# New landing and issue times in the list scheduler of a hybrid SSD / RG-LRU / retention / RWKV-7 block (one Trainium2 core)

## The chip, the cores and the metric

The kernel runs on one core of a Trainium2 chip. The metric is the device time of one execution in microseconds, the median of several runs. The engines are named as in the profile: PE is TensorE (PEld its weight loads), DVE is VectorE, ACT is ScalarE, POOL is GpSimd, SP is SyncE, whose queue (SPq) issues almost all transfers.

## The reference, cut to what matters

One layer over 512 tokens of width 1024, in float32. A combined input projection feeds four token mixers and their gates; the mixer outputs are projected, gated, summed and projected again; a convolutional FFN follows.

```python
def hybrid_mixer(h, w_in, ssm_p, lru_p, ret_p, rwkv_p, w_branch, w_out, cos, sin):
    proj = h @ w_in
    (m_z, m_xbc, m_dt, l_gate, l_x, r_q, r_k, r_v, r_g, rw, gate_logits) = jnp.split(proj, ...)
    y_ssd = mamba2_branch(m_z, m_xbc, m_dt, *ssm_p)
    y_lru = rglru_branch(l_gate, l_x, *lru_p)
    y_ret = retention_branch(r_q, r_k, r_v, r_g, *ret_p, cos, sin)
    y_rwkv = rwkv7_branch(rw, *rwkv_p)
    ys = jnp.stack([y_ssd, y_lru, y_ret, y_rwkv], axis=2)
    branch = jnp.einsum('bsmw,mwd->bsmd', ys, w_branch)
    merged = jnp.sum(jax.nn.sigmoid(gate_logits) * branch, axis=2)
    return merged @ w_out

x = x + hybrid_mixer(rms_norm(x, norm_mix), ...)
x = x + (silu(gt) * val) @ w_down          # val, gt: causal conv of rms_norm(x) @ w_up
return rms_norm(x, norm_final)
```

The RWKV-7 recurrence (a state of 64 x 64 per head, 16 heads) is the sequential part.

## The kernel before, in words

**The products.** Every large product is done in three fp32r matmuls (high x high, high x low, low x high). A weight block of 128 x 1024 floats is loaded by SP (`raw`, L469, three buffers), split on ACT into `whi` (L463) and on DVE into `wlo` (L464), and multiplied by `mm3` (L482, L483, L484) or its counterparts in `proj_tokens` (L603 to L605) and `tail_product` (L1317 to L1319) into an `acc` bank of PSUM, of which there are three. These products are called the large products below.

**The RWKV part.** It goes over eight pairs of heads, j = 0 to 7. `rwkv_a1(j)` makes the projections and decays (L654 to L706). `rwkv_a2(j)` makes 64-token blocks: on DVE and POOL the operands `g` and `bk` (L717 on POOL, L718 to L721 on DVE), on PE their products (L735), on ACT and DVE the masked copies (`ab` L737, `g` L738, `gb` L739), then transposes of `bk` and `v` on PE (L459 `ra<-ident,bk` and `ra<-ident,pv`). A triangular solve follows: `ab` goes through DRAM (`nd` L780, `nt` L783), DVE does 31 steps of two instructions (L789, L791), and the result goes through DRAM again: four writes `xd` (L797), four writes `xtd` (L798), two reads `xr` (L803), four reads `tt` (L806). `rwkv_b(j)` uses it: small matmuls L817 from `xr` and `ab`, a copy on ACT (L821), small matmuls L827 from `tt` and `xr`, a copy on ACT (L830), and then a chain over eight chunks, PE L840, DVE L842, PE L844, ACT L845 and DVE L846, PE L848, DVE L851, and L840 of the next chunk.

**What fills.** Beside the RWKV part stand, in this order of the program, the other mixers (`lru_tiles`, `ret_pair`, `mamba_group`, at last `mamba_finish`), and when they are done and their pool `fl` is closed, `branch` for three of the mixers: it reads the mixer outputs back (`yr`, L1240), splits them (`yh`, `yl`) and does the gate and branch products. The mixer outputs are written to DRAM by `spill` (L609, `y`). After the RWKV part come the last branch, the output product, the FFN and the last norm.

**What sets the order.** The program only lists instructions. At the end of the build `_order` (L406) makes the order of every engine: `_graph` collects dependences, tiles and pools, `_run` (L238) is a list scheduler that plays the program with a duration for each instruction (`_cost`, L115) and takes on each engine the ready instruction of the highest priority; on PE a small matmul that is ready goes before a large product. `_latest` turns the resulting times into new priorities, this is done `_RUNS` = 8 times, and the order with the smallest end is fixed on all engines. The scheduler's times are nowhere in the program; only the order is. For a transfer `_run` has two numbers: how long the issue occupies SP (450 ns before) and when the data has landed (an issue of 450 ns, the bytes at 330 per ns on one shared wire, then 1,500 ns, or 2,500 ns for reads of five kinds of scratch: `xd`, `xtd`, `y`, `ym`, `acd`). For POOL it stretches a two-input DVE instruction that runs beside a POOL one.

Of the kernel before, what the change touches and what calls it, by code (L numbers as in the profile page):

```python
# [66 lines left out]
_RUNS = 8  # L67
_HOP = 60.0
_SWITCH = 500.0
_BACK = 17.0  # L70


def _base(name):
    return name.rsplit("_", 1)[0]
# [163 lines left out]
def _run(g, prio, margin):  # L238


    import heapq
    import types
    E = mybir.EngineType
    ins, N, real = g.ins, g.N, g.real
    left = [len(p) for p in g.preds]
    est, start, done, dur_of = [0.0] * N, [0.0] * N, [0.0] * N, [0.0] * N
    engines = [E.PE, E.DVE, E.Activation, E.Pool, E.SP]
    free = {e: 0.0 for e in engines}
    pend, ready, order = {e: [] for e in engines}, {e: [] for e in engines}, {e: [] for e in engines}
    held, table, wire, was, run = [], "", 0.0, False, 1  # L250
    weights, shorts = [], []
    queue = {t: list(q) for t, q in g.queue.items()}
    room = {t: [(0.0, "")] * b for t, b in g.bufs.items()}
    n_users = {t: len(u) for t, u in g.users.items()}
    pool_left, pool_end = {}, {}
    for t, u in g.users.items():
        pool_left[g.pool_of[t]] = pool_left.get(g.pool_of[t], 0) + len(u)
    behind = {}

    def offer(k):  # L260

        for n in g.news[k]:
            if queue[g.tag_of[n]][0] != n or not room[g.tag_of[n]]:
                return False
            if any(pool_left.get(q, 0) for q in g.gates.get(g.pool_of[n], ())):
                return False
        for n in g.news[k]:
            queue[g.tag_of[n]].pop(0)
            at, old = heapq.heappop(room[g.tag_of[n]])
            est[k] = max(est[k], at)  # L270
            if old:
                behind.setdefault(k, []).append(old)
            for q in g.gates.get(g.pool_of[n], ()):
                est[k] = max(est[k], pool_end.get(q, 0.0))
        heapq.heappush(pend[g.eng[k]], (est[k], k))
        return True

    def try_held():
        again = True
        while again:  # L280
            again = False
            for k in list(held):
                if offer(k):
                    held.remove(k)
                    again = True

    for k in real:
        if not left[k]:
            if g.news[k]:
                held.append(k)  # L290
            else:
                offer(k)
    try_held()
    seq = []
    while len(seq) < len(real):
        best = None
        for e in engines:
            if ready[e] or (e == E.PE and (weights or shorts)):
                t = free[e]
            elif pend[e]:  # L300
                t = max(free[e], pend[e][0][0])
            else:
                continue
            if best is None or t < best[0]:
                best = (t, e)
        t, e = best
        while pend[e] and pend[e][0][0] <= t:
            k = heapq.heappop(pend[e])[1]
            heapq.heappush(ready[e], (-1.0 if g.lead.get(k, k) != k else prio[k], k))
        if e == E.PE:  # L310
            while ready[e]:
                k = heapq.heappop(ready[e])[1]
                heapq.heappush(weights if g.acc[k] else shorts, (-1.0 if g.lead.get(k, k) != k else prio[k], k))
            early = []
            while shorts and shorts[0][0] >= 0 and est[shorts[0][1]] + (300.0 if g.small[shorts[0][1]] else margin) > t:
                early.append(heapq.heappop(shorts))
            if weights and not shorts:
                k = heapq.heappop(weights)[1]
            else:
                if not shorts:  # L320
                    shorts, early = early, []
                    heapq.heapify(shorts)
                k = heapq.heappop(shorts)[1]
            for x in early:
                heapq.heappush(shorts, x)
        else:
            k = heapq.heappop(ready[e])[1]
        i = ins[k]
        dur, tail = g.cost[k]
        if e == E.Activation and type(i).__name__ == "InstActivation":  # L330
            sets = _TABLES.get(str(i.func).split(".")[-1])
            if sets and table not in sets:
                table = sets[0]
                dur += 1283.0
        if e == E.PE:
            if g.small[k] != was:
                was = g.small[k]
                dur += _SWITCH
            if not run and g.acc[k]:
                dur += _BACK  # L340
            run = run + 1 if g.acc[k] else 0
        if e == E.DVE and free[E.Pool] > t and len(i.ins) > 1 and not g.tiles_of[k][-1].startswith(("ra", "rb", "acc")):
            dur *= 1.0 + 0.7 * min(1.0, (free[E.Pool] - t) / dur)
        order[e].append(k)
        seq.append(k)
        start[k], dur_of[k] = t, dur
        free[e] = t + dur
        done[k] = t + dur + tail
        if type(i).__name__ == "InstDMACopy":
            free[e] = t + (450.0 if e == E.SP else 100.0)  # L350
            dur_of[k] = free[e] - t
            wire = max(wire, t + 450.0) + 4.0 * i.outs[0].bass_ap.size() / 330.0
            done[k] = wire + (2500.0 if i.outs[0].bass_ap.tensor.space != bass.MemoryType.DRAM and
                              _base(i.ins[0].bass_ap.tensor.name) in ("xd", "xtd", "y", "ym", "acd") else 1500.0)
        opened = bool(g.news[k])
        for s in g.succ[k]:
            left[s] -= 1
            est[s] = max(est[s], t if k in g.after[s] else t + dur if g.eng[s] == e and e != E.SP else done[k])
            if not left[s]:
                if g.news[s]:  # L360
                    held.append(s)
                    opened = True
                else:
                    offer(s)
        for m in g.tiles_of[k]:
            n_users[m] -= 1
            p = g.pool_of[m]
            pool_left[p] -= 1
            pool_end[p] = max(pool_end.get(p, 0.0), done[k])
            if not n_users[m]:  # L370
                heapq.heappush(room[g.tag_of[m]], (max(done[x] for x in g.users[m]), m))
                opened = True
        if opened:
            try_held()
    return types.SimpleNamespace(order=order, start=start, done=done, dur=dur_of, seq=seq, behind=behind, end=max(done))
# [30 lines left out]
def _order(tc, nc):  # L406

    PE = mybir.EngineType.PE  # L410
    g = _graph(nc)
    first = [float(k + g.N * g.acc[k]) for k in range(g.N)]
    prio, best = first, None
    for n in range(_RUNS):
        r = _run(g, prio, _MARGIN)
        if best is None or r.end < best.end:
            best = r
        late = _latest(g, r, [PE])
        prio = [first[k] if g.eng[k] == PE else late[k] for k in range(g.N)]
    behind = mybir.DependencyInfo(mybir.DependencyClass.NoSync, mybir.DependencyReason.DATA)  # L420
    for seq in best.order.values():
        for a, b in zip(seq, seq[1:]):
            tc.add_manual_dep(g.ins[b], g.ins[a].name, behind, reason="order of issue")
# [1121 lines left out]
```

## Time and profile before

| | |
|---|---|
| runs | 1572.96, 1568.45, 1569.73 us (median 1569.73) |
| profiled execution | 1573.08 us, its span 1571.3 us |
| PE busy | 1532.9 us, 98% |
| DVE / ACT / POOL busy | 1086.4 us, 69% / 734.9 us, 47% / 62.9 us, 4% |
| DMA | 169.46 MB, mean 108 GB/s |
| mean granted PE clock | 0.990 |

The profile is of one execution. Busy PE time counts every moment in which a matmul is under way; matmuls are pipelined, so two that follow each other overlap in the records, and a stretch in which they follow each other slowly is still busy. The distance between starts tells the pace. "DMA a<-b" in a wait means that the transfer's semaphore came last.

### The profile page before, as it was taken

The page shows a single profiled execution, that of the slowest core. Times are in us where ns is not written, and L with a number is a line of the kernel's source. Part 1 is how long each engine was busy: PE and PEld are TensorE (multiplying, and loading weights), DVE is VectorE, ACT ScalarE, POOL GpSimd, SP SyncE. Part 2 cuts the span into 40 slices and gives each one's busy share as a digit, 9 for nine tenths or more (in the row PEclk, how much of TensorE's full clock was granted, in tenths as well). Part 3 has the DMA queues.
Part 4 walks back from the last instruction along what each step waited for, and adds up shares of the span by engine and source line. Part 5 has one row for each costly group of instructions (what it writes and reads, how often), then busy time and mean ns, then how long its engine had stood idle before and what let it go on. Part 6 is the DMA issues. An engine that isn't in the chain of part 4 may idle for free.

```text
span 1571.3 us, 22179 instructions
## 1 busy us (share of the span) xinstructions
PE 1532.9 (98%) x8324; PEld 1286.6 (82%) x8324; DVE 1086.4 (69%) x2334; ACT 734.9 (47%) x1198; POOL 62.9 (4%) x78
## 2 busy tenths in 40 slices
PE   7999999999999999998999999999999999999998
PEld 6888778987888888976888888888888888888886
DVE  6799699897988897897685966435446665655233
ACT  6662577349554686268333423223224444443222
POOL 0000000000100000000000100000000000000000
PEclk9999999999999999998999999999999999999999
DMA  5243234234143243335333432424242322323221
GB/s 197 95 128 94 77 92 121 74 119 118 54 149 101 69 141 105 103 116 161 109 110 93 140 98 85 152 94 134 96 147 82 107 94 96 103 97 107 94 94 67
DMA packets 108460, 169.46 MB, mean 108 GB/s; under 512 B 54832, under 2 KB 64304, under 8 KB 108352
## 3 DMA queue, kind: packets, MB, share of 16 engines
q1 hardware_dynamic: 107632, 166.92, 33.7%
q8 instruction: 66, 1.08, 0.3%
q10 hardware_dynamic: 720, 1.11, 0.2%
q14 instruction: 42, 0.34, 0.1%
HBM read 150.66 MB, written 15.24 MB: 106 GB/s over the span
## 4 chain that ended last, share of the span: by engine, by line
PE 83%; DVE 8%; ACT 3%; DMA 3%; SPq 2%; issue 1%; DVEq 0%; ACTq 0%
PE acc L482 19%; PE acc L484 19%; PE acc L483 19%; PE acc L1319 4%; PE acc L1318 4%; PE acc L1317 4%; PE acc L603 2%; PE acc L604 2%; PE acc L605 2%; PE rb L840 1%; PE ra L735 1%; DVE wlo L464 1%; PE rb L844 1%; PE inn L459 1%; PE ra L459 1%
## 5 line engine op out<-in xcount | busy, mean ns | idle before, releaser
L482 PE MATMUL acc<-hh,whi 128*128 128x512 f32 (+1 forms) x1240 | 493.5, 398 | 2.8 <-ACT hh L527 1.8
L483 PE MATMUL acc<-hh,wlo 128*128 128x512 f32 (+1 forms) x1240 | 494.0, 399 | 0.0
L484 PE MATMUL acc<-hl,whi 128*128 128x512 f32 (+1 forms) x1240 | 490.4, 396 | 0.0
L464 DVE TENSOR_TENSOR wlo<-raw,whi 128x1024 fp32r<-128x1024 f32 x228 | 278.6, 1224 | 243.6 <-PE acc L483 160.8
L463 ACT CAST whi<-raw 128x1024 fp32r<-128x1024 f32 x228 | 238.1, 1046 | 230.6 <-PE acc L1319 84.7
L482 PEld LDWEIGHTS acc<-hh,whi 128*128 128x128 f32 x1240 | 234.6, 189 | 46.6 <-ACT hh L527 2.5
L483 PEld LDWEIGHTS acc<-hh,wlo 128*128 128x128 f32 x1240 | 234.7, 189 | 41.8 <-issue 1.4
L484 PEld LDWEIGHTS acc<-hl,whi 128*128 128x128 f32 x1240 | 234.0, 189 | 42.4 <-issue 1.4
L482 PE MATMUL acc<-yh,whi 128*128 128x512 f32 x256 | 103.3, 403 | 0.0
L483 PE MATMUL acc<-yh,wlo 128*128 128x512 f32 x256 | 102.9, 402 | 0.0
L484 PE MATMUL acc<-yl,whi 128*128 128x512 f32 x256 | 102.4, 401 | 0.0
L1370 ACT ACTIVATE fc<-acc,fw 128x512 f32<-128x512 f32 x44 | 34.4, 782 | 93.2 <-PE acc L484 93.2
L603 PE MATMUL acc<-whi,hh 128*128 128x256 f32 (+1 forms) x256 | 77.8, 304 | 0.0
L604 PE MATMUL acc<-wlo,hh 128*128 128x256 f32 (+1 forms) x256 | 77.1, 301 | 0.0
L605 PE MATMUL acc<-whi,hl 128*128 128x256 f32 (+1 forms) x256 | 77.0, 301 | 0.0
L1317 PE MATMUL acc<-whi,gh 128*128 128x512 f32 x176 | 69.4, 395 | 0.0
L1319 PE MATMUL acc<-whi,gl 128*128 128x512 f32 x176 | 69.4, 395 | 0.0
L1318 PE MATMUL acc<-wlo,gh 128*128 128x512 f32 x176 | 69.4, 395 | 0.0
L1372 DVE SCALAR_TENSOR_TENSOR fc<-acc,fw,fc 128x511 f32<-128x511 f32 x88 | 65.6, 747 | 2.3 <-ACT fc L1370 0.8
L791 DVE TENSOR_TENSOR xr<-xr,prod 128x60 f32<-128x60 f32 (+24 forms) x248 | 58.0, 234 | 7.9
L789 DVE TENSOR_TENSOR prod<-nt,xr 128x60 f32<-128x60 f32 (+24 forms) x248 | 53.7, 217 | 5.1 <-DMA nt<-nd 1.9
L484 PEld LDWEIGHTS acc<-yl,whi 128*128 128x128 f32 x256 | 48.7, 190 | 9.8 <-DVE yl L464 0.2
(335 smaller groups left out, 2458.4 us busy)
## 6 DMA issues: line engine op xcount, KB each, us to landing
raw<-in_wts_dram SPq DMA_DIRECT2D x226, 512.0 KB, 3.3
yr<-y SPq DMA_DIRECT2D x32, 256.0 KB, 2.8
y<-sm SPq DMA_DIRECT2D x24, 256.0 KB, 2.5
nt<-nd SPq DMA_DIRECT2D x32, 128.0 KB, 2.7
sm<-acd SPq DMA_DIRECT2D x16, 256.0 KB, 3.6
x<-in_x_dram SPq DMA_DIRECT2D x4, 512.0 KB, 6.3
sm<-sm SPq DMA_DIRECT2D x32, 64.0 KB, 2.0
ym<-bg SPq DMA_DIRECT2D x16, 128.0 KB, 3.0
```

Of the source, the lines that this page charges most:

```text
L463: nc.scalar.copy(out=hi, in_=src)
L464: nc.vector.tensor_tensor(out=lo, in0=src, in1=hi.bitcast(F32), op=ALU.subtract)
L482: nc.tensor.matmul(ps, wh, xh, start=first, stop=False)
L483: nc.tensor.matmul(ps, wl, xh, start=False, stop=False)
L484: nc.tensor.matmul(ps, wh, xl, start=False, stop=last)
L603: nc.tensor.matmul(o, hh[:, ko, t], wh[:, s], start=ko == 0, stop=False)
L604: nc.tensor.matmul(o, hh[:, ko, t], wl[:, s], start=False, stop=False)
L605: nc.tensor.matmul(o, hl[:, ko, t], wh[:, s], start=False, stop=ko == KT - 1)
L1317: nc.tensor.matmul(ps[i], xh[:, ko, t], w[0][:, s], start=ko == 0, stop=False)
L1318: nc.tensor.matmul(ps[i], xh[:, ko, t], w[1][:, s], start=False, stop=False)
L1319: nc.tensor.matmul(ps[i], xl[:, ko, t], w[0][:, s], start=False, stop=ko == 2 * nblk - 1)
L1372: nc.vector.scalar_tensor_tensor(out=t[:, s:], in0=ps[:, :S - s], scalar=fw[:, o + 2 - s:o + 3 - s], in1=t[:, s:], op0=ALU.mult, op1=ALU.add)
```

## The change

Only `_run` changes, and two tables ahead of it: no instruction of the kernel is added, removed or altered, but a few loads of ACT's function tables, which depend on the order there. Landing: a time for each kind of destination tile (`nt` 2,700 ns, `xd` 2,300, `xtd` 2,400, `xr` 1,900, `ym` 2,300, `tt` 2,600, `bg` 2,500, `yr` 2,000, `sm` 2,100, `nd` 1,600) and 1,700 for all others. Issue on SP: 620 ns for `xd` and `xtd`, 500 for `sm`, 400 for all others. And a two-input POOL instruction is lengthened by what is left of a two-input DVE instruction at its start.

```diff
+_ISSUE = {"xd": 620.0, "xtd": 620.0, "sm": 500.0}
+_LAND = {"nt": 2700.0, "xd": 2300.0, "xtd": 2400.0, "xr": 1900.0, "ym": 2300.0, "tt": 2600.0, "bg": 2500.0, "yr": 2000.0,
+         "sm": 2100.0, "nd": 1600.0}
...
-    held, table, wire, was, run = [], "", 0.0, False, 1
+    held, table, wire, was, run, lock = [], "", 0.0, False, 1, 0.0
...
             dur *= 1.0 + 0.7 * min(1.0, (free[E.Pool] - t) / dur)
+        if e == E.DVE:
+            lock = t + dur if len(i.ins) > 1 and not g.tiles_of[k][-1].startswith(("ra", "rb", "acc")) else 0.0
+        if e == E.Pool and type(i).__name__ == "InstTensorTensor":
+            dur += max(0.0, lock - t)
...
         if type(i).__name__ == "InstDMACopy":
-            free[e] = t + (450.0 if e == E.SP else 100.0)
-            dur_of[k] = free[e] - t
+            name = g.tiles_of[k][0].split("_")[0]
+            dur_of[k] = (_ISSUE.get(name, 400.0) if e == E.SP else 100.0)
+            free[e] = t + dur_of[k]
             wire = max(wire, t + 450.0) + 4.0 * i.outs[0].bass_ap.size() / 330.0
-            done[k] = wire + (2500.0 if i.outs[0].bass_ap.tensor.space != bass.MemoryType.DRAM and
-                              _base(i.ins[0].bass_ap.tensor.name) in ("xd", "xtd", "y", "ym", "acd") else 1500.0)
+            done[k] = wire + _LAND.get(name, 1700.0)
```

In the changed kernel the lines of the instructions stand 7 further down: L817 of before is L824 there, L827 is L834, L840 is L847, L844 is L851, L848 is L855, L482 to L484 are L489 to L491, L603 to L605 are L610 to L612. Rows of the changed order have those numbers; the text uses the numbers of before.

What moves. The first 39 matmuls and the last 1,598 of 7,364 on PE stand as before; nearly everything between them is moved. Three places follow.

The first is PE in `rwkv_a2(3)`, between the products L735 and the transposes of `bk` and `v`. Before:

```order
L604 MATMUL acc<-wlo,hh 128x256
L605 MATMUL acc<-whi,hl 128x256
L735 MATMUL ra<-g,bk 128x128 x8
L459 MATMUL ra<-ident,bk 128x128 x5
L459 MATMUL ra<-ident,pv 128x128
```

In the changed order the last L735 (L742 there) of this pair stands here:

```order
L1138 MATMUL inn<-sm 128x128
L742 MATMUL ra<-g,bk 128x128
L612 MATMUL acc<-whi,hl 128x256
L610 MATMUL acc<-whi,hh 128x256
L611 MATMUL acc<-wlo,hh 128x256
```

Behind it 21 large products follow, the first three of which are shown, before the first transpose of `bk`; before, there was none.

The second is PE in `rwkv_b(4)`, between the small matmuls from `xr` (L817) and those from `tt` (L827). Before:

```order
L605 MATMUL acc<-whi,hl 128x256
L817 MATMUL rb<-xr,ab 32x32 x16
L603 MATMUL acc<-whi,hh 128x256
L1175 MATMUL inn<-bg,sm 128x256
L604 MATMUL acc<-wlo,hh 128x256
L605 MATMUL acc<-whi,hl 128x256
L827 MATMUL rb<-tt,xr 32x32 x16
L840 MATMUL rb<-sv,g 128x64
```

In the changed order it begins so, where L824 is L817:

```order
L824 MATMUL rb<-xr,ab 32x32 x16
L1168 MATMUL inn<-bg,sm 128x64
L611 MATMUL acc<-wlo,hh 128x256
L612 MATMUL acc<-whi,hl 128x256
L610 MATMUL acc<-whi,hh 128x256
```

There are 14 large products of 256 columns between the two groups now, three before. Between L817 and L827 of the eight pairs stood 4, 2, 5, 5, 3, 0, 4 and 4 large products before, and 12, 9, 10, 18, 14, 4, 6 and 6 now.

The third is the passage from `mamba_finish` to `branch`. On PE, before (pair 5 in its `rwkv_b`; `acc<-yh` is the first branch product):

```order
L484 MATMUL acc<-hl,whi 128x512
L817 MATMUL rb<-xr,ab 32x32 x16
L827 MATMUL rb<-tt,xr 32x32 x16
L840 MATMUL rb<-sv,g 128x64 x2
L844 MATMUL rb<-nt,tt 128x128
L848 MATMUL rb<-uv,bt 128x128
L482 MATMUL acc<-yh,whi 128x512
```

And now:

```order
L491 MATMUL acc<-hl,whi 128x512
L851 MATMUL rb<-nt,tt 128x128
L855 MATMUL rb<-uv,bt 128x128
L847 MATMUL rb<-sv,g 128x64 x2
L851 MATMUL rb<-nt,tt 128x128
L855 MATMUL rb<-uv,bt 128x128
L489 MATMUL acc<-yh,whi 128x512
```

Pair 5's L817 and L827 now lie earlier, among the transposes of `mamba_finish`; the passage itself falls between two chunks of pair 5's chain. SP's queue at the same passage, before:

```order
L803 DMA xr<-xd 32x8x32 x2
L469 DMA raw<-in_wts_dram 128x1024 x2
L806 DMA tt<-xtd 32x8x32 x4
L609 DMA y_7_79<-sm 128x512
L609 DMA y_6_78<-sm 128x512
L469 DMA raw<-in_wts_dram 128x1024
L1240 DMA yr<-y_0_80 128x512
```

And now:

```order
L616 DMA y_5_77<-sm 128x512
L616 DMA y_6_78<-sm 128x512
L476 DMA raw<-in_wts_dram 128x1024
L616 DMA y_7_79<-sm 128x512
L1247 DMA yr<-y_0_80 128x512
```

The last write of a mixer output is no longer queued behind the four reads of `tt`. Between the last transpose of `mamba_finish` and the first branch product stood 18 large products on PE before, and stand 15 now. Behind the last instruction of the RWKV part (L858 of pair 7) 799 large products stood before the output product, and 810 stand now.

## Rows read from the trace of the kernel before

**Rows 1.** Page, part 1: busy time by engine, share of the span, instructions.

```profile
PE 1532.9 (98%) x8324; PEld 1286.6 (82%) x8324; DVE 1086.4 (69%) x2334; ACT 734.9 (47%) x1198; POOL 62.9 (4%) x78
```

**Rows 2.** Waits of PE, whole span: us in total, times, longest us.

```profile
PE inn L459 <- DVE nxn L520: 10.2, 1, 10.2
PE rb L827 <- DMA tt<-xtd: 4.8, 3, 3.2
PE ra L459 <- DVE gb L739: 2.4, 2, 2.0
PE rb L844 <- ACT tt L830: 1.9, 2, 1.8
...
PE rb L848 <- DVE uv L846: 1.8, 3, 0.6
PE rb L817 <- DMA xr<-xd: 1.7, 2, 1.1
```

**Rows 3.** Windows: length, PE busy (instructions), granted clock, DMA share, GB/s.

```profile
426.90:434.40 7.50, 5.10 (x28) 0.77 0.45 121
618.20:632.40 14.20, 11.77 (x105) 0.64 0.55 155
733.90:748.40 14.50, 8.81 (x85) 0.65 0.71 232
932.00:939.60 7.60, 7.37 (x83) 0.78 0.58 159
```

**Rows 4.** Timeline, PE, round 629 us and 632 us: start, length; distances tell the pace.

```profile
629.00 0.41 PE L604 MATMUL acc<-wlo,hh 128*128 128x256 f32 x1
629.22 0.41 PE L605 MATMUL acc<-whi,hl 128*128 128x256 f32 x1
...
632.49 0.28 PE L603 MATMUL acc<-whi,hh 128*128 128x256 f32 x1
632.61 0.28 PE L604 MATMUL acc<-wlo,hh 128*128 128x256 f32 x1
```

**Rows 5.** Timeline, passage to `branch`, 733.5 to 744.7 us, PE and SP queue.

```profile
733.54 0.39 PE L483 MATMUL acc<-hh,wlo 128*128 128x512 f32 x1
...
733.76 0.39 PE L484 MATMUL acc<-hl,whi 128*128 128x512 f32 x1
...
735.90 0.85 SPq L609 DMA_DIRECT2D y<-sm  x2
...
738.71 1.22 PE L827 MATMUL rb<-tt,xr 32*32 32x32 f32 x32 [3.21 <-DMA tt<-xtd]
...
740.23 0.79 SPq L1240 DMA_DIRECT2D yr<-y  x2
...
744.62 0.77 PE L482 MATMUL acc<-yh,whi 128*128 128x512 f32 x1
```

**Rows 6.** Timeline, PE, pairs 3 and 6: the waits at L827.

```profile
496.02 0.81 PE L827 MATMUL rb<-tt,xr 32*32 32x32 f32 x32 [1.07 <-DMA tt<-xtd]
...
835.09 0.81 PE L827 MATMUL rb<-tt,xr 32*32 32x32 f32 x32 [0.54 <-DMA tt<-xtd]
```

**Rows 7.** Transfers of tile `tt`: issue to landing, all 32.

```profile
DMA to landing us min/median/max: 1.8/3.1/4.9
```

**Rows 8.** Timeline, PE, transposes side by side (717 us) and among large products (729 us).

```profile
717.82 0.27 PE L459 MATMUL inn<-ident,bg 128*128 128x128 f32 x1
717.92 0.27 PE L459 MATMUL ra<-ident,di 128*128 128x128 f32 x1
...
729.12 0.48 PE L483 MATMUL acc<-hh,wlo 128*128 128x512 f32 x1
...
729.46 0.48 PE L484 MATMUL acc<-hl,whi 128*128 128x512 f32 x1
```

**Rows 9.** Source line L717 (POOL): duration min/median/max in ns.

```profile
L717 POOL TENSOR_TENSOR bk<-pk,di x16: 1291/1635/2250, 69.5 to 871.7; 64x512 f32<-64x512 f32 x16
```

**Rows 10.** Timeline, ACT, one load of a function table.

```profile
740.19 1.28 ACT L1246 ACT_TABLE_LOAD   x1 [1.40 <-DMA y<-sm]
```

## The prediction

> **What bounds the kernel now.** I read the busy times first. PE has work under way in 98% of the span, DVE in 69%, ACT in 47%, POOL in 4% [rows 1]. So only time in which PE stands or runs slowly can come back, and work moved on the other engines counts only where PE waits for it. The next view is what PE waited for [rows 2]. The longest wait, 10.2 us for the first normalised rows, lies in the opening, whose order is kept. The waits behind it are all places of the RWKV part where the order put an instruction on PE before its operand was there: `tt` 4.8 us, `gb` 2.4, the copy L830 1.9, `uv` 1.8, `xr` 1.7. The third view is the granted clock by window: in four windows, each around one of these places, its mean is 0.64 to 0.78 [rows 3], while the mean of the whole span is 0.990. In such a stretch the clock is at 1.2 GHz instead of 2.4, and the reader sees it in the pace: products of 256 columns start 0.22 us apart at 629 us and 0.12 us apart at 632 us [rows 4]. One stretch thus loses 0.10 of each 0.22 us, 45%. PE's work before each fall was thin: a wait, or the small 32 x 32 matmuls of L817 and L827.
>
> **The price of the four places and the two single waits.** The time at half clock in a window is twice its length times what the mean lacks to 1.00 [rows 3].
> - `rwkv_a2(3)`, 426.9 to 434.4: wait for `gb` 2.4 us [rows 2]; clock 2 x 7.5 x 0.23 = 3.5 us, 45% of it 1.6. Together 4.0.
> - `rwkv_b(4)`, 618.2 to 632.4: both waits for `xr`, 1.7 [rows 2]; clock 10.2 us, 45% of it 4.6. Together 6.3.
> - Passage to `branch`, 733.9 to 748.4: waits of 3.2 (`tt`), 1.8 (of the 1.9 for L830) and 0.6 (`uv`) [rows 2]; clock 10.2 us, of which PE waits 2.4, 45% of the rest 3.5. Together 9.1.
> - `rwkv_b(7)`, 932.0 to 939.6: no wait; clock 3.3 us, 45% of it 1.5.
> - L827 of pairs 3 and 6: 1.1 + 0.5 = 1.6 [rows 6].
>
> That is 22.5 us, all that this change can sensibly get.
>
> **What the change does there, part by part.**
>
> *Landing and issue times.* The scheduler expected `xtd` to land after 1.5 us and now 2.4, an `xd` or `xtd` issue to hold SP for 0.45 us and now 0.62; with eight such issues ahead, `tt` is expected later by about 0.9 + 8 x 0.17 = 2.3 us against the end of the solve. So PE's order keeps large products for that time. In pair 4 there are 14 of 256 columns (14 x 0.12 = 1.7 us) between L817 and L827 where there were three; in pairs 3 and 6, 18 and 6 where there were 5 and 4; in pair 7, 6 for 4. The waits at L827 were 1.1 and 0.5 us [rows 6], and two further products of 512 columns, 0.22 us each [rows 5], or 13 of 256 cover them. The waits at L817 in pair 4 are not covered by products behind them; they go if L817 is placed later against the solve, which the longer issue times do. I take back all of `rwkv_b(4)`, 6.3, of pair 7, 1.5, and of the single waits, 1.6.
>
> *`rwkv_a2(3)`.* Between the last L735 and the transposes stand 21 products of 256 columns now, 21 x 0.12 = 2.5 us, against none; the wait was 2.4. I take back 4.0.
>
> *The passage.* This hole is moved, not closed. Before, the last product ahead of it started at 733.76 and, at 0.22 each, ended near 733.98; the first branch product started at 744.62 [rows 5]: 10.6 us without a large product, in which PE did little. What ended it is a path through DRAM: the last two `y` writes were issued from 735.90, `yr` was read from 740.23, the product came at 744.62, 8.7 us in all, and the writes stood on SP behind the reads of `tt`. Now they don't, which takes some 2 us off; the 8.7 us stay, and 15 products (3.4 us) instead of 18 stand ahead of the hole. I put the new hole at 5 to 7 us with about 1 us of chain work in it, and half of the clock's price; 6.5 of the 9.1 us stay lost, 2.6 come back. Its ends: 0 back if the clock falls as long as before and the writes are late for another reason, 9.1 if the other small matmuls hide it.
>
> *Fewer interruptions.* Merging small matmuls looks like a gain and is none: a transpose beside another takes 0.10 us (717.82 to 717.92), and one between two large products lengthens their distance to 0.34 (729.12 to 729.46), 0.12 more than the 0.22 of products alone [rows 5, 8]. The 0.02 between them, on some 50 places, is 1 us at most; costed at nothing.
>
> *POOL.* Its lengthened instruction takes 1.29 to 2.25 us, 16 times [rows 9]; PE waits for none of them, and POOL is busy 4% [rows 1]. Nothing. If DVE's `bk` behind it were late, PE's L735 would wait at most the spread, 0.96 us, in some pairs.
>
> *ACT.* Four more table loads of 1.28 us [rows 10], 5.1 us on an engine busy 47% [rows 1]; nothing, and 5.1 us if every one stood ahead of L821 or L830, for which PE waits.
>
> *The end.* 810 large products stand behind the RWKV part; a longer chain there is covered by 180 us of products.
>
> *New waits.* An order changed in 5,700 matmuls makes some of its own. Bounds: nothing, and as much as the old ones, 22.5. I take 3, the size of a wait such as that for `gb` [rows 2] with a little clock, since the lengths that made the old ones are now nearer to the trace.
>
> **Sum.** 4.0 + 6.3 + 1.5 + 1.6 + 2.6 - 3 = 13.0 us. Against the profiled execution, 1573.1, that is 1560.1; that execution lies 3.4 us above the median of the runs, 1569.7, so the median should be **1556.7 us**, rounded to 1557.
>
> **Rivals.**
>
> *The waits move to other places (about 1569).* One landing time stands for all transfers of a kind, but `tt` landed after 1.8 to 4.9 us, median 3.1 [rows 7]. Where it comes 1.8 us late, PE waits as before: four pairs of eight give 7.2 us, with one long fall of the clock (4.6) 11.8, which eats the 13. For it speaks the spread; against it that the waits of before sat where products were missing, in three pairs of eight. The Trainium skill (DMA: Bandwidth & Descriptors, Latency and other measured facts) gives the access time of HBM as 0.2 us on average and 2 us at high load, and calls it the main part of a transfer's fixed cost. By that rule no constant per kind can be right, and the outcome would be this rival's; the spread of `tt` agrees, and whether load causes it no row here shows.
>
> *Slower, by the clock (about 1578).* The 64 small matmuls of L817 and L827 remain in each of eight pairs, and the clock fell around three of these groups: pairs 4, 5 and 7 [rows 3]. If the new neighbours (longer runs of transposes beside L735 and L817, and the hole at the passage) made it fall in all eight for 10.2 us each, that is 8 x 4.6 = 36.8 us against the 4.6 + 3.5 + 1.5 of before, 27 worse; less the 14 us of waits at most that go, 13 slower; with six falls some 4 slower. It decides from six falls on; I put it at 8 slower. Against it: large products now stand between L817 and L827 everywhere, which is what pairs 0 to 3 and 6 had when the clock held. The Trainium skill (TensorE: Matmul & The Clock Gate, HAM oscillation) says that an array that idles at a transfer in every step of a loop is slowed again in each step. By that rule this rival would be right if every pair waited; the four windows agree that falls follow thin work.
>
> *It does nothing (1569.7).* The scheduler keeps the best of eight plays, so another set of times could give an order no better on the chip. But the places named are changed in the order itself, so I count this in the first rival.
>
> **How the numbers follow.** The forecast, that most of the four places is recovered, gets 0.64; waits that move, 0.23; slower, 0.13. The range goes down to all 22.5 us recovered, 1547, and up over the first rival to a little over the median, 1571; the slower case and a gain beyond the four places are left out, 2 in 10. A measurement of this kernel can tell 0.3% (4.7 us) from no change: faster means under 1565.0, slower over 1574.4. The forecast less its worst ends lies under 1565: faster 0.64, same 0.23, slower 0.13.
>
> **What would show it.** Right: PE's waits for `tt`, `xr` and `gb` under 3 us together (8.9 before); at most two falls of the clock inside the span, one at the passage, and a mean clock of 0.995 or more; a hole of 5 to 7 us before the first branch product. Wrong: waits for `tt` or `xr` at pairs that had none, three or more long falls, or a new wait of PE for ACT or DVE above 2 us. The forecast fails altogether if PE's waits outside the opening sum to 20 us again.

## The result and the profile after

| | before | after |
|---|---|---|
| median of five runs each | 1572.46 us | 1579.77 us (1576.71 to 1585.89) |
| profiled execution, its span | 1573.08, 1571.3 us | 1579.09, 1577.3 us |
| mean granted PE clock | 0.990 | 0.992 |

The ratio, reckoned from all runs and not as the quotient of the two medians, is 1.0058, interval 1.0042 to 1.0074: slower by 0.6%, or 7.3 us in the medians, where 13 us of gain were forecast. (In these runs the kernel before lies 2.7 us above the median of the three runs shown ahead of the prediction.)

The busy times by engine, page of the kernel after:

```profile
PE 1532.2 (97%) x8324; PEld 1284.8 (81%) x8324; DVE 1086.9 (69%) x2334; ACT 737.6 (47%) x1202; POOL 61.8 (4%) x78
```

They are those of [rows 1] within 3 us: the engines have the same work, but for ACT's four further table loads (2.7 us more). PE's waits, whole span of the kernel after (us in total, times, longest):

```profile
PE inn L466 <- DVE nxn L527: 10.4, 1, 10.4
PE rb L855 <- DVE uv L853: 3.2, 4, 1.3
PE ra L466 <- ACT di L688: 3.0, 3, 1.9
PE inn L466 <- ACT sm L1056: 2.6, 1, 2.6
PE acc L489 <- ACT hh L534: 1.9, 2, 1.5
PE acc L489 <- ACT sm L972: 1.8, 1, 1.8
PE acc L611 <- DVE wlo L471: 1.7, 2, 1.0
PE rb L834 <- DMA tt<-xtd: 1.4, 1, 1.4
PE inn L466 <- DVE mtmp L1174: 1.3, 2, 0.7
PE rb L824 <- DMA xr<-xd: 1.1, 2, 0.9
PE ra L466 <- DVE gb L746: 1.1, 2, 0.8
PE rb L851 <- ACT tt L837: 1.0, 1, 1.0
```

Against [rows 2] two things are to be seen. The waits for transfers fell, `tt` from 4.8 to 1.4 us and `xr` from 1.7 to 1.1, and so did the one for `gb` (made on DVE), from 2.4 to 1.1. And there are new or longer waits for ACT and DVE: `uv` 3.2 for 1.8, `di` 3.0, `sm` 2.6 and 1.8 (for 0.5), `wlo` 1.7. Over all rows of the view, the opening's `nxn` left out, PE waited 6.5 us for transfers and 13.9 us for ACT and DVE before, and 2.5 and 24.7 us now.

The windows of the kernel after (length; PE, PEld, DVE, ACT and POOL busy; clock; DMA share; GB/s):

```profile
141.00:147.00 6.00, 5.80 (x81) 5.31 (x81) 4.37 (x5) 2.32 (x6) 2.91 (x2) 0.72 0.61 134
216.00:221.00 5.00, 3.17 (x14) 2.29 (x14) 4.64 (x14) 4.96 (x6) 0.00 (x0) 1.00 0.37 141
...
425.00:433.00 8.00, 6.65 (x52) 5.97 (x51) 7.96 (x11) 5.24 (x11) 0.00 (x0) 1.00 0.35 106
471.00:482.00 11.00, 9.07 (x47) 7.83 (x47) 10.56 (x28) 4.13 (x6) 0.00 (x0) 0.84 0.30 35
...
605.00:622.00 17.00, 15.12 (x144) 13.35 (x143) 9.33 (x17) 13.84 (x26) 0.00 (x0) 0.90 0.49 135
694.00:704.00 10.00, 7.42 (x27) 5.55 (x26) 7.94 (x34) 3.73 (x6) 0.00 (x0) 0.83 0.19 73
738.00:762.00 24.00, 21.38 (x106) 17.52 (x105) 14.40 (x31) 14.76 (x25) 3.41 (x2) 0.86 0.48 163
930.00:940.00 10.00, 10.00 (x72) 8.15 (x71) 3.25 (x6) 1.35 (x3) 0.00 (x0) 1.00 0.58 139
```

The rows at 425, 605, 738 and 930 us are the four places of [rows 3]: `rwkv_a2(3)` and `rwkv_b(7)` have the full clock now (so has 940 to 950 us, into which the second reaches), `rwkv_b(4)` and the passage lose less than before. The rows at 141, 471 and 694 us are places where before there was no fall. Each has, as the first four had, a wait or a group of the small 32 x 32 matmuls of L817 and L827 in it. Such a place alone does not bring a fall: from 216 to 221 us PE has work under way in 3.17 of 5 us, and the clock stays at 1.00.

The three longest new stalls, timeline of the kernel after (start, length; PE and ACT):

```profile
217.65 0.39 PE L491 MATMUL acc<-hl,whi 128*128 128x512 f32 x1
219.87 0.50 PE L489 MATMUL acc<-hh,whi 128*128 128x512 f32 x1 [1.83 <-ACT sm L972]
...
217.93 1.28 ACT L972 ACT_TABLE_LOAD   x1
219.22 0.60 ACT L972 ACTIVATE sm<-acc 128x512 f32<-128x512 f32 x1
...
474.06 0.49 PE L466 MATMUL inn<-ident,sm 128*128 128x128 f32 x3
476.48 0.33 PE L466 MATMUL ra<-ident,di 128*128 128x128 f32 x1 [1.93 <-ACT di L688]
...
696.71 0.39 PE L491 MATMUL acc<-hl,whi 128*128 128x512 f32 x1
699.68 1.11 PE L466 MATMUL inn<-ident,sm 128*128 128x128 f32 x4 [2.58 <-ACT sm L1056]
```

PE stands for 1.83, 1.93 and 2.58 us, where starts in a dense stretch are 0.1 to 0.2 us apart. At 217.65 the next `acc` bank is not free: ACT L972 has to read it, and stands behind a table load. At 476.48 PE's next transpose has waited for the chain that makes `di`, at 699.68 for `sm` from ACT. None of these is a transfer.

### The profile page after: what moved, and what is told of

It is laid out like the page before. It is cut to its first block, busy times and chain, and to the rows that moved or that the text cites. A ratio compares the mean times of both kernels' runs of the same rounds, so it can differ in the third digit from the quotient of the medians.

```text
span 1577.3 us, 22194 instructions
## 1 busy us (share of the span) xinstructions
PE 1532.2 (97%) x8324; PEld 1284.8 (81%) x8324; DVE 1086.9 (69%) x2334; ACT 737.6 (47%) x1202; POOL 61.8 (4%) x78
## 4 chain that ended last, share of the span: by engine, by line
PE 82%; DVE 9%; ACT 3%; DMA 2%; SPq 2%; issue 2%; DVEq 0%; ACTq 0%
PE acc L489 19%; PE acc L490 19%; PE acc L491 19%; PE acc L1325 4%; PE acc L1326 4%; PE acc L1324 4%; PE rb L847 1%; PE ra L742 1%; PE acc L611 1%; PE acc L612 1%; PE acc L610 1%; DVE sm L929 1%; PE rb L851 1%; PE rb L855 1%; DVE wlo L471 1%
## 5 line engine op out<-in xcount | busy, mean ns | idle before, releaser
L489 PE MATMUL acc<-hh,whi 128*128 128x512 f32 (+1 forms) x1240 | 492.7, 398 | 4.0 <-ACT hh L534 1.9
L491 PE MATMUL acc<-hl,whi 128*128 128x512 f32 (+1 forms) x1240 | 491.2, 397 | 0.0
L489 PEld LDWEIGHTS acc<-hh,whi 128*128 128x128 f32 x1240 | 235.2, 190 | 49.0 <-ACT hh L534 2.5
L491 PEld LDWEIGHTS acc<-hl,whi 128*128 128x128 f32 x1240 | 234.7, 190 | 42.0 <-issue 1.4
L489 PE MATMUL acc<-yh,whi 128*128 128x512 f32 x256 | 102.6, 401 | 0.0
L491 PE MATMUL acc<-yl,whi 128*128 128x512 f32 x256 | 101.5, 397 | 0.2 <-DVE yl L471 0.2
L612 PE MATMUL acc<-whi,hl 128*128 128x256 f32 (+1 forms) x256 | 76.9, 301 | 0.0
L610 PE MATMUL acc<-whi,hh 128*128 128x256 f32 (+1 forms) x256 | 76.5, 300 | 0.0
L929 DVE SCALAR_TENSOR_TENSOR sm<-acc,cp,sm 128x511 f32<-128x511 f32 (+2 forms) x72 | 53.7, 745 | 4.4 <-ACT sm L927 2.8
L491 PEld LDWEIGHTS acc<-yl,whi 128*128 128x128 f32 x256 | 48.5, 189 | 9.6 <-DVE yl L471 0.5
```

The lines of the kernel that those rows point to most:

```text
L489: nc.tensor.matmul(ps, wh, xh, start=first, stop=False)
L491: nc.tensor.matmul(ps, wh, xl, start=False, stop=last)
L610: nc.tensor.matmul(o, hh[:, ko, t], wh[:, s], start=ko == 0, stop=False)
L612: nc.tensor.matmul(o, hl[:, ko, t], wh[:, s], start=False, stop=ko == KT - 1)
L929: nc.vector.scalar_tensor_tensor(out=t[:, s:], in0=ps[:, :S - s], scalar=cp[:, o + taps - 1 - s:o + taps - s], in1=t[:, s:], op0=ALU.mult, ...
```

## The experiments

The scheduler in the kernel prints nothing, but the end of its chosen play, called its own end here, can be read when the order is made. It is a plan and no chip time. For the kernel before the eight plays ended at 1570.6, 1556.1, 1555.1, **1548.6**, 1564.1, 1571.0, 1566.5 and 1568.7 us; with the new numbers at 1583.8, **1556.4**, 1560.7, 1561.8, 1577.7, 1568.0, 1571.9 and 1581.3. PE stands for 23.7 us in the first plan and 31.1 us in the second, and the three stalls above are in the second plan too, as 2.1 us at 214.8, 2.6 at 472.4 and 3.1 at 687.4. So the scheduler itself held the new order to be 7.8 us longer than the old one, each by its own numbers.

Theories: A, the time follows the own end; B, C and D, the loss comes from the landing times, the rule for POOL or the issue times; F, any altered number draws another order, and the pair before and after is two draws.

### Each part alone and in pairs

All six edits undo parts of the change. Landing alone (the other parts as before):

```diff
-        if e == E.Pool and type(i).__name__ == "InstTensorTensor":
-            dur += max(0.0, lock - t)
...
-            dur_of[k] = (_ISSUE.get(name, 400.0) if e == E.SP else 100.0)
+            dur_of[k] = (450.0 if e == E.SP else 100.0)
```

Issue alone keeps the old landing expression instead (1,500 and 2,500 ns) and drops the POOL rule:

```diff
-            done[k] = wire + _LAND.get(name, 1700.0)
+            done[k] = wire + (2500.0 if i.outs[0].bass_ap.tensor.space != bass.MemoryType.DRAM and
+                              _base(i.ins[0].bass_ap.tensor.name) in ("xd", "xtd", "y", "ym", "acd") else 1500.0)
```

The POOL rule alone has both `450.0` and the old landing; the pairs are made from the same lines. What was expected of the landing times alone:

> Only the table of landing times of the change; issue times and the POOL rule as before. Theory A (the measured time follows the end that the scheduler itself reckons for the order it fixes: 1548.6 us for the order of before, 1556.4 for the changed one, 1555.2 for this one): 6.6 us over before, ratio 1.004, some 1579. Rival B (the later landing times themselves are the loss, whatever the search finds): all of it, 7 us over before. Rival C (the POOL rule is the loss): as before, 1572. Rival D (the issue times are the loss): as before.

Of the issue times alone:

> Only the issue times of the change. Theory A (the scheduler's own end is 1555.2 us against 1548.6 for before): 6.6 us over before, some 1579. Rival B (landing times): as before, 1572. Rival C (POOL rule): as before. Rival D (issue times): 7 us over before.

Of the rule for POOL alone:

> Only the longer POOL instruction of the change. Theory A (own end 1548.4 us against 1548.6): as before within 1.5 us, 1571 to 1574. Rival B (landing times) and D (issue times): as before too. Rival C (the POOL rule): 7 us over before, 1579.

Of landing and issue times without the rule for POOL:

> Landing and issue times of the change without the POOL rule. Theory A (own end 1551.9 us against 1548.6): 3.3 us over before, ratio 1.002, some 1576, so less than with either of its two parts alone. Rivals B and D (landing or issue times cost by themselves): at least 7 us over before, and no less than the larger of the two parts. Rival C (POOL rule): as before.

Of landing times with the rule for POOL:

> Landing times and POOL rule of the change, issue times as before. Theory A (own end of the scheduler 1552.9 us, 4.3 over before): 4 us over before, 1577. Theory F (a redraw: each set of numbers sends the eight plays to another order, and what one part costs in one company it doesn't in another): no sum of parts holds; anywhere from 2 us under to 27 over before. Rival C (the POOL rule costs 6 to 9 us in any company): 27 + 6 = 33 us over before, 1605.

Of issue times with the rule for POOL:

> Issue times and POOL rule of the change, landing times as before. Theory A (own end 1550.2 us, 1.6 over before): 2 us over before, 1574. Theory F (redraw): anywhere from 2 us under to 27 over before, not the sum. Rival C (the POOL rule costs 6 to 9 us in any company): 4 + 6 = 10 us over before, 1583.

Measured, ratio to the kernel before on the same chip:

| parts in | own end, us | median, us | ratio (interval) |
|---|---|---|---|
| landing | 1555.2 | 1599.52 | 1.0183 (1.0164 to 1.0201) |
| issue | 1555.2 | 1576.62 | 1.0021 (1.0008 to 1.0034) |
| POOL rule | 1548.4 | 1578.62 | 1.0039 (1.0024 to 1.0054) |
| landing, issue | 1551.9 | 1570.87 | 0.9986 (0.9975 to 0.9997) |
| landing, POOL rule | 1552.9 | 1578.91 | 1.0049 (1.0035 to 1.0063) |
| issue, POOL rule | 1550.2 | 1574.48 | 1.0009 (0.9999 to 1.0019) |
| all three (the change) | 1556.4 | 1579.77 | 1.0058 (1.0042 to 1.0074) |

The ratios here too are reckoned from all runs. The parts do not add up. Landing alone costs 27 us, with issue it gains 2, with the rule for POOL it costs 6. No part carries the loss in every company, so B, C and D fall. A is right in the trend at most: two orders with the same own end, 1555.2, lie 23 us apart. PE's waits of the landing-only kernel, its longest rows behind the opening's:

```profile
PE rb L822 <- DMA xr<-xd: 8.7, 5, 2.8
PE rb L464 <- DVE ab L880: 4.8, 2, 4.6
PE rb L853 <- DVE uv L851: 4.0, 5, 1.7
PE acc L487 <- ACT sm L970: 2.9, 1, 2.9
```

Here the order puts L817's counterpart (L822) too early in five places. The greater part of its loss is the clock: the profiled execution, 1606.3 us, has a mean of 0.977, which by the prediction's price (2 x 1604.6 x 0.023, 45% of it) is 33 us lost against 14 before, 19 more; its waits outside the opening are 34.9 us against 20.4, 14.5 more. Together that is the 33 us by which the two profiled executions differ.

### Redraws without any of the change

The kernel before with its third play fixed instead of the best one; no number is altered:

```diff
-        if best is None or r.end < best.end:
+        if n == 2:
```

> The kernel before with all its numbers, except that the order of the third of the eight plays is fixed, not that of the best (own end 1555.1 us against 1548.6). Theory A: 6.5 us over before, 1579. Theory F (redraw): off by several us in either direction, more likely slower. Rivals B, C, D (the new numbers are the loss): as before, 1572, since none of them is in it.

Measured: 1588.26 us, 1.0101 (1.0086 to 1.0116). PE's waits of this kernel, longest rows behind the opening's:

```profile
PE rb L848 <- DVE uv L846: 6.9, 5, 2.5
PE acc L482 <- ACT sm L965: 5.1, 2, 4.9
PE acc L482 <- ACT sm L1052: 5.0, 1, 5.0
```

And the kernel before with one old number moved by 0.1 us:

```diff
-                              _base(i.ins[0].bass_ap.tensor.name) in ("xd", "xtd", "y", "ym", "acd") else 1500.0)
+                              _base(i.ins[0].bass_ap.tensor.name) in ("xd", "xtd", "y", "ym", "acd") else 1600.0)
```

> The kernel before with one number altered that hardly matters for what is true of the transfers: 1,600 ns instead of 1,500 for the landing of all but the five kinds. Own end 1554.8 us. Theory A: 6 us over before, 1578. Theory F (redraw): off by several us in either direction, more likely slower. Rivals C and D: as before, 1572.

Measured: 1586.38 us, 1.0089 (1.0074 to 1.0103). Two redraws that have nothing to do with the change cost 16 and 14 us, twice what the change cost, and with the same sort of wait: ACT, DVE and full banks. Their own ends, 1555.1 and 1554.8 us, lie 6.5 and 6.2 us above that of before, so A accounts for less than half of either loss. So a loss of 7 us from one redraw says nothing of the new numbers: F stands. The plans also say where the kernel before stands. Moving its 1,500 ns by -60 to +100 ns, in ten values, gives own ends of 1547.2 to 1554.8 us; with 1548.6 it had, by the plan, one of the better draws of its kind. Of these only the last was timed.

Then the changed kernel with one number moved, chosen because its own end is as low as that of before:

```diff
-         "sm": 2100.0, "nd": 1600.0}
+         "sm": 1500.0, "nd": 1600.0}
```

> The changed kernel with one number moved: the landing of `sm` 1,500 ns for 2,100. The scheduler's own end is 1548.4 us, as low as that of the kernel before (1548.6) and 8.0 lower than that of the change. Theory A (time follows the scheduler's own end, about 25 us above it, the median over the ten orders timed so far): 1570 to 1575 us, level with before and some 6 below the change. Theory F (any redraw of the order; the own end says nothing): anywhere from 1571 to 1600 us, like the eight redraws timed so far, and more likely above before than level with it.

Measured: 1571.52 us, 0.9998 (0.9987 to 1.0009), as A has it, and at the lower edge of what F allows (1571 to 1600): with another draw of the new numbers, one of the same own end as before, the loss of the change is gone.

### Taking the luck of the draw out

To compare the numbers and not two draws, the order was searched further with each set: a shift of up to 1.5 us on a random twentieth of the priorities off PE is kept if the own end falls, 3,900 to 8,000 plays for each kernel (the expectation below says 3,000, which is too few), and the kept shifts are written into the kernel:

```diff
+_SEEDS = [
...
-    for n in range(_RUNS):
+    for n in range(4):
...
-            best = r
+            best, base = r, prio
...
+    for seed in _SEEDS:
+        rnd = random.Random(seed)
+        base = [base[k] + (rnd.uniform(-1500.0, 1500.0) if rnd.random() < 0.05 else 0.0) * (g.eng[k] != PE) for k in range(g.N)]
+    best = _run(g, base, _MARGIN)
```

Theory E, formed here: the new numbers are nearer to the chip, so with about equal search (the last shifts kept were found after some 6,400 to 7,800 plays in all six orders of the two full sets) their plans keep better there. All new numbers:

> The changed kernel's numbers, but the order is searched further: some 3,000 further plays, each with random shifts of the priorities off PE, keep the lowest end; own end 1541.2 us for 1556.4. Theory A: 15 us of own end come back on the chip, 1564 to 1567 us, faster than before by 5 or more. Theory F: 1571 to 1590 us. Theory E (the numbers themselves matter once the luck of eight plays is taken out; those of the change are nearer to the chip, so its plan is kept better): the excess over the own end is smaller here than in the order searched with the old numbers, 20 to 25 us against 28 to 32.

All old numbers:

> The kernel before with its own numbers, searched in the same way (random shifts of the priorities off PE, 68 of them kept); own end 1537.5 us for 1548.6. Theory A: 1561 to 1565 us. Theory F: 1571 to 1590 us. Theory E: 1565 to 1570 us, the mean excess of orders made with the old numbers (24, 33 and 32 us) over the own end, and so no faster than the order searched with the new numbers although its own end is 3.7 us lower.

Landing and issue times, without the rule for POOL (rarer and larger shifts, as in the third order of each set below: one in fifty, up to 3 us):

> New landing and issue times without the rule for POOL, searched in the same way (56 shifts kept); own end 1538.4 us for 1551.9. Theory A: 1561 to 1565 us, 6 to 10 below the 1570.9 of the unsearched order. Theory F: 1571 to 1590 us. Theory E: as the order searched with all new numbers, 19 to 25 us over the own end, 1557 to 1563 us.

After 1560.31 and 1572.91 us for the first two, two further orders of each set, from other shifts, were to tell numbers from luck:

> The new numbers once more, searched with other random shifts; own end 1541.8 us. Theory E (the new numbers keep the plan better on the chip: 19 to 24 us over the own end): 1560 to 1566 us. Theory F2 (the 12 us between the first two searched orders were the luck of one order each; excess 20 to 40 us whatever the numbers): 1562 to 1582 us, and not ordered by the numbers.

> The old numbers once more, searched with other random shifts; own end 1539.0 us. Theory E (excess with the old numbers some 32 to 36 us): 1571 to 1575 us. Theory F2: 1559 to 1579 us, as likely below the orders searched with the new numbers as above.

> The new numbers, searched with rarer and larger shifts; own end 1542.1 us. Theory E: 1561 to 1566 us. Theory F2: 1562 to 1582 us.

> The old numbers, searched with rarer and larger shifts; own end 1537.9 us. Theory E: 1570 to 1574 us. Theory F2: 1558 to 1578 us.

At last the landing times alone and the issue times alone, searched:

> The new landing times alone (issue as before, no rule for POOL), searched as the others; own end 1536.0 us. If the landing times carry the better plan (theory E1): excess over the own end as with all new numbers, 13 to 23 us, 1549 to 1559 us. If they carry none of it (E2): excess as with the old numbers, 29 to 35 us, 1565 to 1571 us. The unsearched order with these times alone took 44 us more than its own end; if that was their fault and no bad draw (E3), the searched one lies above 1575 us.

> The new issue times alone (landing as before, no rule for POOL), searched as the others; own end 1538.8 us. If the issue times carry the better plan (E2): 13 to 23 us over the own end, 1552 to 1562 us. If the landing times do (E1): 29 to 35 us, 1568 to 1574 us. Both about 26 us would mean that the two share it, 1565 us here.

Measured; the excess is the median less the own end:

| searched with | own end | median, us | excess | ratio to before (interval) | clock, median of the runs |
|---|---|---|---|---|---|
| new, 1st | 1541.2 | 1560.31 | 19.1 | 0.9923 (0.991 to 0.9937) | 0.994 |
| new, 2nd | 1541.8 | 1554.73 | 12.9 | 0.988 (0.9861 to 0.9899) | 0.9975 |
| new, 3rd | 1542.1 | 1560.76 | 18.7 | 0.9927 (0.9908 to 0.9947) | 0.995 |
| old, 1st | 1537.5 | 1572.91 | 35.4 | 1.0002 (0.9985 to 1.0019) | 0.9895 |
| old, 2nd | 1539.0 | 1569.49 | 30.5 | 0.9975 (0.9958 to 0.9992) | 0.993 |
| old, 3rd | 1537.9 | 1566.97 | 29.1 | 0.9961 (0.9946 to 0.9976) | 0.993 |
| landing, issue | 1538.4 | 1561.78 | 23.4 | 0.9934 (0.992 to 0.9948) | 0.9935 |
| landing | 1536.0 | 1561.91 | 25.9 | 0.993 (0.9908 to 0.9951) | 0.9945 |
| issue | 1538.8 | 1558.53 | 19.7 | 0.9909 (0.9892 to 0.9925) | 0.9955 |

The slowest order with the new numbers, 1560.8 us, is faster than the fastest with the old ones, 1567.0, although the old ones promise ends 3.6 us lower on average. The means are 1558.6 and 1569.8 us: 11.2 us for the new numbers. If the numbers did not matter, three against three would fall out so in one case of 20; the three orders with a part of the new numbers, 1558.5 to 1561.9 us, lie below all three old ones too. So E stands against F2, the luck of one order each, but in the order of the two sets and not in its sizes: six of its seven ranges were missed, by 0.2 to 5.3 us, and within one set the orders differ by 6 us. Its premise holds in the trace of the kernel before for the issue times: an `xd` issue held SP for 0.62 us in the median, as the new number has it, and not for 0.45. For the landing times it holds in part at most (see "Why 3 was wrong"). Most of the new landing numbers are longer than the old ones, and no order was made with numbers that are merely longer; so that the new numbers keep better is shown, and that they do it by being nearer to the chip is not. A does not hold from one set of numbers to the other: by its 25 us the old numbers' orders should have taken 1563. Nor do its sizes hold within the old set: longer search took 10 to 11 us off the plan and 0 to 6 off the chip.

Where the 11 us are, by the second order of each set. With the old numbers (span and clock; busy times; PE's waits, longest rows):

```profile
core 0: 1569.5 us, clock 0.992
```

```profile
PE 1530.0 (97%) x8324; PEld 1284.7 (82%) x8324; DVE 1087.9 (69%) x2334; ACT 731.5 (47%) x1196; POOL 60.8 (4%) x78
```

```profile
PE inn L465 <- DVE nxn L526: 13.9, 1, 13.9
PE rb L833 <- DMA tt<-xtd: 6.1, 6, 2.0
PE rb L854 <- DVE uv L852: 3.0, 4, 1.5
PE acc L490 <- DVE yl L470: 1.6, 1, 1.6
PE rb L823 <- DMA xr<-xd: 1.6, 3, 0.8
```

With the new numbers:

```profile
core 0: 1551.5 us, clock 0.997
```

```profile
PE 1520.1 (98%) x8324; PEld 1278.2 (82%) x8324; DVE 1085.3 (70%) x2334; ACT 736.3 (47%) x1201; POOL 64.5 (4%) x78
```

```profile
PE inn L472 <- DVE nxn L533: 12.3, 1, 12.3
PE ra L472 <- ACT di L694: 1.8, 2, 1.1
PE rb L857 <- issue: 1.7, 3, 0.9
PE acc L495 <- ACT sm L978: 1.2, 1, 1.2
PE rb L840 <- DMA tt<-xtd: 1.2, 1, 1.2
```

PE waits for `tt` in six places and for `xr` in three with the old numbers, for `tt` in one and for `xr` in none with the new ones. Over the three orders of each set PE's waits for transfers are 6.1, 7.7 and 4.5 us against 3.9, 1.2 and 3.2, on average 3.3 us more. But its other waits, `nxn` left out, are 10.5, 10.6 and 9.1 us against 12.1, 10.2 and 14.6, on average 2.2 us less: of the waits 1.1 us are left. The median clocks differ by 0.0037 on average, which by the prediction's price is 2 x 1565 x 0.0037 x 0.45 = 5.2 us. Together 6.3 of the 11.2 us. The busy times agree that waits are the smaller part: PE has work under way for 1533.2, 1530.0 and 1526.1 us against 1524.4, 1520.1 and 1521.9, on average 7.6 us more, and the spans of these profiled executions differ by 9.2. So most of the gain is work that runs faster, by the clock above all; what the rest is, no row names.

Which part carries it: the issue times alone keep as well as all parts (19.7 us of excess), the landing times alone lie between (25.9). One order each, where three of one set spread over 6 us, makes the issue times the likelier carrier, and no more than that. The landing times alone are no fault in themselves: searched, the kernel that took 1599.5 us takes 1561.9. The rule for POOL alone was not searched and run.

The second order with all new numbers, 1554.73 us (0.988), is faster than the kernel before and the change.

## Why the prediction was wrong

**The step that failed is "New waits": "I take 3".** Set against its own terms:

| term | forecast back, us | after, lost there still | back, us |
|---|---|---|---|
| `rwkv_a2(3)` | 4.0 | waits 0.27 and 0.98, no fall | 2.7 |
| `rwkv_b(4)` | 6.3 | waits 1.39 and 0.49, half clock 3.4 us | 2.9 |
| passage | 2.6 | PE idle 2.6, half clock 6.7 us | 3.9 |
| `rwkv_b(7)` | 1.5 | nothing | 1.5 |
| single waits at L827 | 1.6 | nothing | 1.6 |
| new waits and falls elsewhere | -3 | see below | -17.0 |

The half clock is priced as in the prediction; at the passage about 0.9 us of it is wait. The places that the prediction named gave 12.6 of the 16.0 us it wanted from them: `rwkv_b(4)` was to come back whole, but PE waits there 1.39 us for `tt`, for which this pair had not waited before. Elsewhere PE waited 9.1 us before (20.4 us over all rows without `nxn`, less 11.3 at the named places) and waits 21.5 now (27.2 less 5.7), and the three new falls at 141, 471 and 694 us are 10.3 us at half clock, 4.6 lost: 12.4 + 4.6 = 17.0. The sum is 4.4 us of loss, and the profiled executions differ by 6.0.

**Why 3 was wrong.** It was a price for a few fresh waits, but nearly the whole order between the first 39 and the last 1,598 matmuls was drawn anew. Both orders are the best of eight plays, but that of before was by its plan a good draw (1548.6 us) and the new one a worse (1556.4); the four places were what was left of the good one. Taking its bad places away and keeping its good ones was never on offer. The prediction's own upper bound, 22.5 us, held the true value, 17.0; it was put aside because "the lengths that made the old ones are now nearer to the trace". Of the issue times that is so. Of the landing times it is not, taken together; issues of the kernel before (count, KB each, median us from issue to landing):

```profile
yr<-y SPq DMA_DIRECT2D x32, 256.0 KB, 2.8
...
xtd<-prod SPq DMA_DIRECT2D x32, 32.0 KB, 2.0
...
xd<-xr SPq DMA_DIRECT2D x32, 16.0 KB, 2.3
xr<-xd SPq DMA_DIRECT2D x16, 32.0 KB, 2.0
```

With its 450 ns of issue, the bytes and the landing number, the scheduler had 3.75 us for `yr` and now has 3.25, and 3.05 and 2.45 for `xr`: nearer. For `xtd` it had 2.05 and now has 2.95, for `xd` 2.0 and 2.8: farther. And nearer numbers would not decide how one draw turns out, as the redraws show. The new order's worst stalls could have been seen without a chip, since the plan has them.

**The passage.** The hole is there as forecast. Timeline of the kernel after (PE and SP queue):

```profile
750.78 0.40 PE L491 MATMUL acc<-hl,whi 128*128 128x512 f32 x1
...
756.89 0.77 PE L489 MATMUL acc<-yh,whi 128*128 128x512 f32 x1
...
748.45 0.32 SPq L616 DMA_DIRECT2D y<-sm  x1
750.56 0.80 SPq L1247 DMA_DIRECT2D yr<-y  x2
```

From the end of the last product, near 751.0, to the first branch product are 5.9 us, forecast 5 to 7, 10.6 before [rows 5]. From the last `y` write to that product are 8.4 us; from the first of the last two they were 8.7 before, so the path through DRAM stayed much as it was.

**Landing.** The transfers of `tt` in the kernel after, issue to landing:

```profile
DMA to landing us min/median/max: 1.8/4.1/5.3
```

The median of before was 3.1 [rows 7]; reckoned from the issue as above, the new number of 2.6 says 3.15, the old one 3.05. The same transfer of the same size lands, in the median, 1 us later in another order. The Trainium skill (DMA: Bandwidth & Descriptors, Latency and other measured facts) ties the time to load, and the prediction took from it that no constant per kind can be right. The spread agrees with that; whether load causes it, no run here shows. The rival that stood beside it, that waits for transfers come back, did not come true: they fell from 6.5 to 2.5 us, and in the orders searched with all new numbers, with a constant per kind, they are 1.2 to 3.9.

**The rivals.** The one nearest to what happened is "It does nothing": it says that the scheduler keeps the best of eight plays, so that another set of times could give an order no better on the chip. The prediction counted it in the first rival and gave it neither a price below zero nor a chance of its own, since the named places change in the order itself. They do, and the rest of the order changes with them. "Slower, by the clock" asked for falls at the groups of L817 and L827 of six or more pairs. There are five falls inside the span (four before), two of them at or right behind such groups (141 and 605 us), and the mean clock rose from 0.990 to 0.992. So the sign of that rival came out, not its mechanism. (Its price is off too: the waits of the named places sum to 11.3 us, not 14, so that eight falls would give 16 us and not 13.) Of what was to show the forecast right, only the hole of 5 to 7 us came: PE's waits for `tt`, `xr` and `gb` are 3.6 us, not under 3, and the mean clock is 0.992, not 0.995. Of what was to show it wrong, there are five falls and a new wait for ACT of 2.6 us. The sign the prediction gave as its condition of failure, PE's waits outside the opening at 20 us again, came out as well: 24.7 + 2.5 us without `nxn`, of which `hh` in the opening is 1.5.

**ACT and POOL.** POOL's 61.8 us are those of before within 1.1, as said. A table load now stands directly ahead of an eviction that PE waits for, at 217.93 us, and costs 1.28 of the 1.83 us of that wait: inside the bound of 5.1 us that the prediction gave and set aside.

## What to carry to other kernels

A heuristic scheduler that keeps the best of a few plays is a draw: altering any of its numbers redraws the order, and here redraws that had nothing to do with the change moved the time by up to 16 us, more than the 11 us that the numbers were worth in the searched orders. Judge its numbers by several orders searched equally far with each set, by how much the chip adds to the plan, and not by one pair; and before forecasting, read the new plan's own end and the stalls that stand in it. What a better model is worth shows only together with more search: here the numbers alone lost 7 us in the one draw that was the change, the search alone gave 0 to 6, and both together gave 12 to 18.

## What the runs showed of the hardware that had not been expected

One order does not take one time. The third order searched with the old numbers took 1561.0 to 1572.3 us in twelve runs, with a granted clock of 0.996 in the fastest and 0.990 in the slowest; 0.006 of the clock is 2 x 1566 x 0.006 x 0.45 = 8.5 of the 11.3 us by the price above. The four runs of the fastest order lie within 2.0 us at 0.997 to 0.998. So one order meets falls of the clock in some runs and not in others. What makes an order liable to it is not shown: PE's waits in the profiled execution of that order, 13.6 us outside the opening, are no more than the 17.8 us of the third order searched with the new numbers, whose five runs lie within 3.4 us. The profile alone hides the spread: the profiled execution of that order, 1561.0 us, was its fastest, and looks like the new numbers' orders.
